# Late stages of a gated hybrid layer: three sets of places for split weights, split two units ahead

## The chip, the cores and the metric

One core of one Trainium2 chip runs the kernel. The metric is the device time in microseconds of one execution. Five engines work side by side, each through its own instructions in order: TensorE (PE, matmuls and its weight loads), VectorE (DVE), ScalarE (ACT), GpSimd (POOL) and SyncE (SP, which here only issues transfers). Matmuls write PSUM, which has eight banks of 128 x 512 floats; everything else stands in SBUF.

## What is computed

One decoder layer on 512 positions of width 2048, in float32. Three token mixers share one input projection; each result is multiplied by SiLU of its gate path, projected back, weighted by a sigmoid gate and summed:

```python
hn = rms_norm(x, norm_gain)
proj = hn @ w_in            # queries, keys, values, z gates, and 3 x 2048 gate_logits
ua = (ya * silu(za)) @ w_branch_a
ub = (yb * silu(zb)) @ w_branch_b
uc = (yc * silu(zc)) @ w_branch_c
g = sigmoid(gate_logits.reshape(b, s, 3, 2048))
y = g[:, :, 0] * ua + g[:, :, 1] * ub + g[:, :, 2] * uc
return x + y @ w_out
```

## The kernel before

**Precision.** Every float32 operand is split into a high piece (ACT's cast to the fast float32 format, "hi") and a low piece (DVE's subtraction of hi from the original, "lo"). A product is three matmuls into one PSUM bank: x-high by w-high, x-low by w-high, x-high by w-low.

**The late stages**, from 714 us on, are a list of units, `late.units`, run one after another by `Late.run`:
- Gates: six blocks (three gates, two halves of 1024 columns). A block is a 2 x 2 block product done with seven products in place of eight. Eight units "FIRST" (F0 to F7 below: products P1, P5, P6, P4, 24 matmuls each), then eight units "SECOND" (S0 to S7: P2, P7, P3, 18 matmuls). Each product has two PSUM banks (two halves t), filled over eight units. In the eighth, each finished product is taken over ("evacuated") by DVE additions into R (`first_1`, `second_2`), P1 by ACT. `tags` rotates the four pairs of banks: in the next block P5 takes the banks of P2, P6 those of P7, and P4 those of P3.
- Branches: four column groups, each branch B (3 units), A (3), C (2), 24 matmuls a unit. In a branch's last unit DVE multiplies by the gate values g, which come back from memory. Four PSUM banks are used in turn with four.
- Output: left block (SECOND, then FIRST), right block (FIRST, then SECOND).

**A unit's weights.** `load` fetches them into a raw tile (three in all); `sums` makes block sums in place on DVE (three subtractions for FIRST, one for SECOND); `early` has ACT cast the first half (P1 and P5, or P2 and P7), hi0; `split` has DVE make lo0 and ACT cast the second half, hi1; lo1 follows on DVE. In before there are two sets of places for each half: hi0 and lo0 in tags a and c, hi1 and lo1 in b and wd.

**The order is written by hand.** `mm` counts matmuls; each third one is a tick, half a slot. `later(dt, f)` puts f's instructions into the engines' queues dt slots on. So an instruction's place in the queue of DVE or ACT is fixed by its slot, and it waits there in order, together with all behind it. SP's order is made by the compiler. Before, in unit i: load of i+3 and split of i+1 at its start, sums of i+2 half a slot in, early of i+2 two slots in.

**Other steps.** `gates.finish` has ACT do a sigmoid on R and store it to memory (four in each block). `plan_x` starts the late units from the stage before. `Branch.split` also fetched, for a branch's first unit, the gate tiles g into four places of a ring that R uses too (`r_tile`).

Of the kernel before, what the change touches and what calls it, by code (L numbers as in the profile page):

```python
# [13 lines left out]
F32R = mybir.dt.float32r  # L14
# [5 lines left out]
P = 128  # L20
# [23 lines left out]
def tile_hybrid_block(ctx, tc, xT, x, memT, mem, ng, mng, w_in, b_forget, gqa, gka, sinks, gqb, gkb, gqc, gkc,  # L44
                      w_mem, w_a, w_b, w_c, w_out, relm, out):
    nc = tc.nc
    ve, ac, po, pe, sy = nc.vector, nc.scalar, nc.gpsimd, nc.tensor, nc.sync
# [7 lines left out]
    def f32(ap):  # L55
        return ap.bitcast(F32)
# [9 lines left out]
    def place(n, name, dtype=F32):  # L66

        return yp.tile([P, 2, S], dtype, tag=f"ys{n}", name=name)
# [43 lines left out]
    gdr = [nc.dram_tensor(f"gates_{i}", (S, D), F32, kind="Internal").ap() for i in range(3)]  # L112
# [9 lines left out]
    def at_slot(t, f):  # L122

        heapq.heappush(agenda, (t, next(seq), f))

    def later(dt, f):
        at_slot(clock[0] + dt, f)
# [42 lines left out]
    def w_tile(which, dtype=F32R):  # L170

        return wp.tile([P, 2, 512], dtype, tag=f"w{which}", name=f"w{which}{cnt[0]}")
# [33 lines left out]
    def bank(i, name):  # L206
        return ps.tile([P, 512], F32, tag=TAGS[i], name=name)
# [92 lines left out]
    early = tc.tile_pool(name="early", bufs=1)  # L300
# [247 lines left out]
    def split(dst_hi, dst_lo, src):  # L548
        ac.copy(dst_hi, src)
        def low():  # L550
            ve.tensor_tensor(dst_lo, src, f32(dst_hi), op=ALU.subtract)
            release("T")
        later(0.5, low)
# [411 lines left out]
    gp = []  # L965
# [6 lines left out]
    def tiles_of(t):  # L972

        return slice(t * P, (t + 1) * P), slice(2 * P + t * P, 2 * P + (t + 1) * P)
# [3 lines left out]
    def r_tile(name):  # L978
        ring["R"] += 1
        return place((0, 1, 2, 6)[ring["R"] % 4], f"{name}_{ring['R']}")  # L980
# [9 lines left out]
    def parts(hi, lo, src, dt=0.5):  # L990
        ac.copy(hi, src)
        later(dt, lambda: ve.tensor_tensor(lo, src, f32(hi), op=ALU.subtract))

    def x_tiles(u, name):
        ax[u] = tuple(cp.tile([P, 4, 256], F32R, tag=f"a{p}{u}", name=f"x{p}{name}{u}") for p in "hl")
        return ax[u]

    def y_tiles(u, name):
        ay[u] = tuple(gp[0].tile([P, 3, 256], F32R, tag=f"b{p}{u}", name=f"y{p}{name}{u}") for p in "hl")
        return ay[u]  # L1000
# [34 lines left out]
    class Late:  # L1035
# [11 lines left out]

        def run(self, lo, hi):
            for i in range(lo, hi):
                self.step("load", i + 3)  # L1050
                self.step("split", i + 1)
                later(0.5, lambda: self.step("sums", i + 2))
                later(2, lambda: self.step("early", i + 2))
                self.units[i].run()

    late = Late()
    wcnt = [0]

    def raw_tile():
        wcnt[0] += 1  # L1060
        return gp[0].tile([P, 4, 512], F32, tag="raw", bufs=3, name=f"rawl{wcnt[0]}")

    def halves():

        n = wcnt[0]
        return ((w_tile("a"), w_tile("c")), (w_tile("b"), gp[0].tile([P, 2, 512], F32R, tag="wd", bufs=2, name=f"wd{n}")))

    def mm(count, *args, **kw):
        pe.matmul(*args, **kw)  # L1069
        count[0] += 1  # L1070
        if count[0] % 3 == 0:
            tick()

    class Product:
# [27 lines left out]

        def half(self, n):

            hi, lo = halves()[n]
            some = sorted(wa for m, xa, wa in (SECOND if self.second else FIRST)[2 * n:2 * n + 2])
            k = len(some)
            src = self.raw[:, some[0]:some[-1] + 1:max(some[-1] - some[0], 1), :]
            ac.copy(hi[:, :k, :], src)  # L1109
            for i, wa in enumerate(some):  # L1110
                self.w[wa] = (hi[:, i, :], lo[:, i, :])
            return lambda: ve.tensor_tensor(lo[:, :k, :], src, f32(hi[:, :k, :]), op=ALU.subtract)  # L1112
# [3 lines left out]

        def split(self):
            self.low()
            later(1.5, self.half(1))

        def run(self):
            u = self.u
# [101 lines left out]
    def plan_x(left):  # L1224


        def alpha(u):
            xs = place(2 + u % 2, f"xa{u}").rearrange("p k (t n) -> p (k t) n", t=2)
            sy.dma_start(out=xs, in_=xad[u * P:(u + 1) * P, :].rearrange("p (k n) -> p k n", n=256))
            later(5, lambda: parts(*x_tiles(u, "x"), xs, 1))  # L1230

        def beta(u):
            if u % 2 == 0:
                beta.t = raw_tile()
            xs = beta.t[:, 2 * (u % 2):2 * (u % 2) + 2, :].rearrange("p k (t n) -> p (k t) n", t=2)[:, 0:3, :]
            sy.dma_start(out=xs, in_=xbd[u * P:(u + 1) * P, :].rearrange("p (k n) -> p k n", n=256))
            later(5, lambda: parts(*y_tiles(u, "x"), xs, 1))
        t0 = left - 32
        for u in range(NP):
            later(max(0, t0 - 16 + 2.5 * u), lambda u=u: beta(u))  # L1240
            later(t0 - 0.5 + 4 * u, lambda u=u: alpha(u))
        for dt, what, i in ((11, "load", 0), (15, "load", 1), (19, "load", 2), (21, "sums", 0), (23, "sums", 1), (25, "sums", 2),
                            (28, "early", 0)):
            later(t0 + dt, lambda what=what, i=i: late.step(what, i))
        later(left - 2.5, lambda: late.step("split", 0))
        later(left - 0.5, lambda: late.step("early", 1))

    def gates(gi, cpair):
        c = cpair * 1024

        def finish(h, t, r):
            def fin():
                ac.activation(r, r, AF.Sigmoid)
                ac.dma_start(out=gdr[gi][tiles_of(t)[h], c:c + 1024].rearrange("p (a n) -> p a n", a=2), in_=r)
            later(4, fin)
        turn = 3 * (len(late.units) // (2 * NP))
        tags = [(turn + n) % 4 for n in range(4)]
        b = Blocks(w_in, GATE + gi * D + c, (tags, tags), finish)
        b.plan(0, b.first_1)
        b.plan(1, b.second_2)  # L1260
# [7 lines left out]
    BR = (("B", w_b, 3, 1, 0), ("A", w_a, 3, 0, 3), ("C", w_c, 2, 2, 6))  # L1268
# [21 lines left out]
    class Branch:  # L1290
# [15 lines left out]

        def split(self):
            br, w, npair, gi, base = BR[self.bi]
            self.hi, self.lo = halves()[(self.cg * 8 + base + self.p) % 2]
            parts(self.hi, self.lo, self.raw[:, 0:2, :], 1)  # L1310
            if self.p == 0:
                for i in range(2):
                    t = r_tile(f"g{br}")
                    sy.dma_start(out=t, in_=gdr[gi][i * 2 * P:(i + 1) * 2 * P, self.cg * 512:(self.cg + 1) * 512]
                                 .rearrange("(b p) n -> p b n", p=P))
                    self.g[2 * i], self.g[2 * i + 1] = t[:, 0, :], t[:, 1, :]

        def run(self):
            br, w, npair, gi, base = BR[self.bi]
            xh, xl = y_split[base + self.p]  # L1320
            first, last = self.p == 0, self.p == npair - 1
            if first:
                self.banks["tags"] = tags = ((2, 3), (0, 1))[ucnt[0] % 2]
                for b in range(4):
                    self.banks[b] = bank(tags[b // 2], f"u{br}{self.cg}_{b}")
                ucnt[0] += 1
            count = [0]
            for b in range(4):
                c = slice(b * P, (b + 1) * P)
                for k in range(2):  # L1330
                    for i, (x, wt) in enumerate(((xh, self.hi), (xl, self.hi), (xh, self.lo))):
                        mm(count, self.banks[b], x[:, k, c], wt[:, k, :], start=(first and k == 0 and i == 0),
                           stop=(last and k == 1 and i == 2))
                if last:
                    self.evac(b)
            if self.cg == 3 and last and self.bi == 0:
                plan_y()
# [18 lines left out]
    def plan_y():  # L1356

        def one(u):
            xs = blocks(place(3 + u % 2, f"ya{u}"))
            sy.dma_start(out=xs, in_=yad[u * P:(u + 1) * P, :].rearrange("p (k n) -> p k n", n=256))  # L1360
            later(5, lambda: parts(*x_tiles(u, "y"), xs, 1))
        for u in range(6):
            later((1, 3, 8, 10, 15, 17)[u], lambda u=u: one(u))
# [34 lines left out]
    for cg in range(4):  # L1398
        for bi, (br, w, npair, gi, base) in enumerate(BR):
            banks, g = {}, {}  # L1400
# [5 lines left out]
    def outputs(cpair, tags):  # L1406
        c = cpair * 1024
        cols = slice(c, c + 1024)

        def finish(h, t, r):  # L1410
            (ac if h else sy).dma_start(out=out[tiles_of(t)[h], cols].rearrange("p (a n) -> p a n", a=2), in_=r)
        return Blocks(w_out, c, tags, finish, resid=x)

    left = outputs(0, ((1, 2, 3, 0), (2, 3, 0)))
# [101 lines left out]
```

## Time and profile before

| | us |
|---|---|
| median of 3 runs | 1533.58 (1532.06 to 1534.87) |
| the profiled execution | 1534.17 |
| its span, first to last instruction | 1532.4 |
| PE busy in the span | 1492.3 |
| DVE busy | 1083.6 |
| ACT busy | 721.6 |

A matmul's end is modelled, so successive rows overlap; the pace is read from the starts. "Idle before" is the time an engine stood before a row, with what ended the wait.

### The profile page before, as it was taken

The page shows a single profiled execution, that of the slowest core. Times are in us where ns is not written, and L with a number is a line of the kernel's source. Part 1 is how long each engine was busy: PE and PEld are TensorE (multiplying, and loading weights), DVE is VectorE, ACT ScalarE, POOL GpSimd, SP SyncE. Part 2 cuts the span into 40 slices and gives each one's busy share as a digit, 9 for nine tenths or more (in the row PEclk, how much of TensorE's full clock was granted, in tenths as well). Part 3 has the DMA queues.
Part 4 walks back from the last instruction along what each step waited for, and adds up shares of the span by engine and source line. Part 5 has one row for each costly group of instructions (what it writes and reads, how often), then busy time and mean ns, then how long its engine had stood idle before and what let it go on. Part 6 is the DMA issues. An engine that isn't in the chain of part 4 may idle for free.

```text
span 1532.4 us, 20507 instructions
## 1 busy us (share of the span) xinstructions
PE 1492.3 (97%) x7233; PEld 1273.4 (83%) x7233; DVE 1083.6 (71%) x1818; ACT 721.6 (47%) x1198; POOL 272.0 (18%) x295
## 2 busy tenths in 40 slices
PE   8999999999999999999999999999999999999998
PEld 7999999998877888888887878787878788887876
DVE  7576765663577764568878877777777556589987
ACT  5434654663566654454444444435355322245432
POOL 3323760662225431200000000000000101110000
PEclk9999999999999999999999999999999999999999
DMA  6656433223244322476666676767676756567583
GB/s 198 172 187 207 122 109 111 84 76 93 83 146 158 99 72 78 162 235 210 210 202 221 206 230 197 243 192 246 193 228 208 278 194 198 173 229 259 191 294 140
DMA packets 125264, 273.23 MB, mean 178 GB/s; under 512 B 13916, under 2 KB 52956, under 8 KB 125160
## 3 DMA queue, kind: packets, MB, share of 16 engines
q1 hardware_dynamic: 120984, 257.22, 52.6%
q10 hardware_dynamic: 4176, 14.69, 3.0%
q8 instruction: 57, 0.93, 0.2%
q14 instruction: 47, 0.39, 0.1%
HBM read 240.39 MB, written 31.48 MB: 177 GB/s over the span
## 4 chain that ended last, share of the span: by engine, by line
PE 73%; DVE 11%; ACT 6%; DMA 5%; issue 3%; POOL 1%; ACTq 1%; SPq 0%; DVEq 0%; POOLq 0%
PE P L1069 27%; PE z L284 11%; PE uA L1069 4%; PE qA L284 4%; PE kB L284 3%; PE qB L284 3%; PE uB L1069 3%; PE kvA L284 3%; PE uC L1069 3%; DMA rawl<-in_w_in_dram 3%; PE qC L284 3%; PE vB L284 2%; DVE R L1003 2%; DVE rawl L1006 2%; DVE wd L1112 2%
## 5 line engine op out<-in xcount | busy, mean ns | idle before, releaser
L1109 ACT CAST wa<-rawl 128x1024 fp32r<-128x1024 f32 x128 | 134.7, 1052 | 256.2 <-PE P L1069 140.1
L198 DVE TENSOR_TENSOR wc<-wa,wb 128x512 fp32r<-128x512 f32 (+2 forms) x254 | 162.0, 664 | 109.3 <-ACT wb L195 108.7
L195 ACT CAST wb<-wa 128x512 fp32r<-128x512 f32 (+2 forms) x254 | 131.3, 565 | 143.8 <-PE z L284 48.3
L1006 DVE TENSOR_TENSOR rawl<-rawl 128x512 f32<-128x512 f32 x256 | 176.6, 690 | 26.6 <-DMA rawl<-in_w_in_dram 16.5
L1112 DVE TENSOR_TENSOR wc<-rawl,wa 128x1024 fp32r<-128x1024 f32 x128 | 156.3, 1221 | 50.8 <-ACT wa L1109 50.7
L1350 POOL TENSOR_TENSOR y<-y,gA 128x512 f32<-128x512 f32 x16 | 24.8, 1559 | 701.0 <-DVE gA L1348 700.4
L1109 ACT CAST wb<-rawl 128x512 fp32r<-128x512 f32 (+1 forms) x128 | 107.1, 837 | 74.7 <-PE P L1069 51.7
L1112 DVE TENSOR_TENSOR wd<-rawl,wb 128x512 fp32r<-128x512 f32 (+1 forms) x128 | 121.8, 952 | 12.9 <-ACT wb L1109 12.7
L284 PE MATMUL z<-ah,wb 128*128 128x512 f32 x256 | 102.2, 399 | 0.0
L284 PE MATMUL z<-ah,wc 128*128 128x512 f32 x256 | 100.0, 391 | 0.0
L284 PE MATMUL z<-al,wb 128*128 128x512 f32 x256 | 99.8, 390 | 0.0
L1069 PE MATMUL P<-wd,xhx 128*128 128x512 f32 x192 | 76.5, 398 | 4.0 <-DVE wd L1112 3.6
L1069 PE MATMUL P<-wb,xhx 128*128 128x512 f32 x192 | 75.9, 395 | 1.8 <-ACT wb L1109 1.0
L1069 PE MATMUL P<-wb,xlx 128*128 128x512 f32 x192 | 74.9, 390 | 0.0
L1069 PE MATMUL P<-wa,xlx 128*128 128x512 f32 x192 | 74.7, 389 | 0.0
L1069 PE MATMUL P<-wa,xhx 128*128 128x512 f32 x192 | 74.7, 389 | 0.0
L1069 PE MATMUL P<-wa,yhx 128*128 128x512 f32 x192 | 74.7, 389 | 0.0
L1069 PE MATMUL P<-wa,ylx 128*128 128x512 f32 x192 | 74.7, 389 | 0.0
L1069 PE MATMUL P<-wc,yhx 128*128 128x512 f32 x192 | 74.7, 389 | 0.0
L1069 PE MATMUL P<-wc,xhx 128*128 128x512 f32 x192 | 74.7, 389 | 0.0
L1003 DVE TENSOR_TENSOR R<-P,R 128x512 f32<-128x512 f32 x88 | 56.1, 684 | 20.6 <-PE P L1069 20.2
L574 POOL TENSOR_SCALAR pB<-pB,denB 128x128 f32<-128x128 f32 (+3 forms) x48 | 56.1, 1169 | 49.1 <-DVE denB L573 34.5
(384 smaller groups left out, 4022.1 us busy)
## 6 DMA issues: line engine op xcount, KB each, us to landing
rawl<-in_w_in_dram SPq DMA_DIRECT2D x144, 512.0 KB, 4.4
rawl<-in_w_out_dram SPq DMA_DIRECT2D x48, 512.0 KB, 4.7
wa<-in_w_in_dram SPq DMA_DIRECT2D x63, 384.0 KB, 3.3
wa<-in_w_in_dram SPq DMA_DIRECT2D x64, 256.0 KB, 3.1
rawl<-in_w_in_dram SPq DMA_DIRECT2D x48, 256.0 KB, 4.2
gates<-R ACTq DMA_DIRECT2D x24, 512.0 KB, 7.9
wa<-in_w_in_dram SPq DMA_DIRECT2D x16, 512.0 KB, 3.7
wa<-in_w_mem_dram SPq DMA_DIRECT2D x16, 512.0 KB, 3.4
```

Of the source, the lines that this page charges most:

```text
L195: ac.copy(hi[:, :n], raw[:, i, :n])
L198: ve.tensor_sub(lo[:, :n], raw[:, i, :n], f32(hi[:, :n]))
L284: pe.matmul(pb, a, m, start=b in fresh, stop=last and not todo[b])
L574: po.tensor_scalar(p, p, den[:, 4 + i:5 + i], None, op0=ALU.mult)
L1003: ve.tensor_tensor(out, a, b, op=ALU.add)
L1006: ve.tensor_tensor(out, a, b, op=ALU.subtract)
L1069: pe.matmul(*args, **kw)
L1109: ac.copy(hi[:, :k, :], src)
L1112: return lambda: ve.tensor_tensor(lo[:, :k, :], src, f32(hi[:, :k, :]), op=ALU.subtract)
L1350: po.tensor_tensor(y, y, g, op=ALU.add)
```

## The change

Three sets of places for each half: the first half takes tags a and c for two units of three and both tiles of b for the third; the second half takes new tags wd and we with three tiles each. Per unit i, load is put in for i+4, early for i+2 at the start, split of i+2 one slot in, sums of i+3 two and a half slots in. Branch gate values are fetched by a step of their own, one slot into a branch's last unit but one. A gate block's sigmoids come 3 slots after the evacuation in place of 4. The first units' steps in `plan_x` are moved to suit.

```diff
             for i in range(lo, hi):
-                self.step("load", i + 3)
-                self.step("split", i + 1)
-                later(0.5, lambda: self.step("sums", i + 2))
-                later(2, lambda: self.step("early", i + 2))
+                self.step("load", i + 4)
+                self.step("early", i + 2)
+                later(1, lambda i=i: self.step("split", i + 2))
+                later(2.5, lambda i=i: self.step("sums", i + 3))
                 self.units[i].run()
...
-    def halves():
-
-        n = wcnt[0]
-        return ((w_tile("a"), w_tile("c")), (w_tile("b"), gp[0].tile([P, 2, 512], F32R, tag="wd", bufs=2, name=f"wd{n}")))
+    hcnt = [0, 0]
+
+    def half_tiles(n):
+
+        hcnt[n] += 1
+        if n == 1:
+            return tuple(gp[0].tile([P, 2, 512], F32R, tag=f"w{i}", bufs=3, name=f"w{i}{hcnt[1]}") for i in "de")
+        return (w_tile("b"), w_tile("b")) if hcnt[0] % 3 == 0 else (w_tile("a"), w_tile("c"))
...
-            hi, lo = halves()[n]
+            hi, lo = half_tiles(n)
...
             self.low()
-            later(1.5, self.half(1))
+            later(1, self.half(1))
...
         for dt, what, i in ((11, "load", 0), (15, "load", 1), (19, "load", 2), (21, "sums", 0), (23, "sums", 1), (25, "sums", 2),
-                            (28, "early", 0)):
+                            (27.5, "early", 0), (28.5, "split", 0), (30, "early", 1), (31.5, "load", 3), (32.5, "split", 1)):
             later(t0 + dt, lambda what=what, i=i: late.step(what, i))
-        later(left - 2.5, lambda: late.step("split", 0))
-        later(left - 0.5, lambda: late.step("early", 1))
...
-            later(4, fin)
+            later(3, fin)
...
-            self.hi, self.lo = halves()[(self.cg * 8 + base + self.p) % 2]
+            self.hi, self.lo = half_tiles((self.cg * 8 + base + self.p) % 2)
             parts(self.hi, self.lo, self.raw[:, 0:2, :], 1)
-            if self.p == 0:
-                for i in range(2):
...
+        def fetch_g(self):
+            br, w, npair, gi, base = BR[self.bi]
+            for i in range(2):
+                t = r_tile(f"g{br}")
...
+            if self.p == npair - 2:
+                later(1, self.fetch_g)
```

## Rows read from the trace of the kernel before

**Rows 1.** The page, busy time of the engines, share of the span, instructions.

```profile
PE 1492.3 (97%) x7233; PEld 1273.4 (83%) x7233; DVE 1083.6 (71%) x1818; ACT 721.6 (47%) x1198; POOL 272.0 (18%) x295
```

**Rows 2.** Timeline of PE: start, duration, engine, line, what; in brackets idle time and releaser.

```profile
786.31 0.39 PE L1069 MATMUL P<-wa,yhx 128*128 128x512 f32 x1
786.54 0.39 PE L1069 MATMUL P<-wa,ylx 128*128 128x512 f32 x1
...
794.11 0.50 PE L1069 MATMUL P<-wb,xhx 128*128 128x512 f32 x1 [0.16 <-DVE R L1003]
794.45 0.40 PE L1069 MATMUL P<-wb,xlx 128*128 128x512 f32 x1
```

**Rows 3.** PE's waits from 714 us on: sum, times, longest.

```profile
PE P L1069 <- DVE wd L1112: 7.2, 10, 1.7
PE uA L1069 <- DVE wc L992: 2.4, 1, 2.4
PE P L1069 <- ACT wb L1109: 1.0, 5, 0.2
PE P L1069 <- DVE R L1003: 0.8, 5, 0.2
```

**Rows 4.** Stretches: length, PE's busy time (matmul records), granted clock, DMA share, GB/s.

```profile
714.30:790.30 76.00, 76.00 (x337) 1.00 0.67 215
793.00:820.00 27.00, 26.02 (x110) 1.00 0.75 242
...
950.30:977.30 27.00, 25.30 (x107) 1.00 0.72 236
```

**Rows 5.** Timeline of PE, last gate block, branches and output.

```profile
1180.26 0.39 PE L1069 MATMUL P<-wa,yhx 128*128 128x512 f32 x1
...
1209.12 0.50 PE L1069 MATMUL uA<-wc,ysh 128*128 128x512 f32 x1 [2.41 <-DVE wc L992]
...
1406.52 0.50 PE L1069 MATMUL P<-wd,xhy 128*128 128x512 f32 x1 [1.71 <-DVE wd L1112]
...
1467.37 0.50 PE L1069 MATMUL P<-wd,xhy 128*128 128x512 f32 x1 [0.71 <-DVE wd L1112]
...
1479.67 0.50 PE L1069 MATMUL P<-wd,xhy 128*128 128x512 f32 x1 [1.13 <-DVE wd L1112]
```

**Rows 6.** Timeline of DVE, the same stretches.

```profile
1181.14 0.69 DVE L1003 TENSOR_TENSOR R<-P,R 128x512 f32<-128x512 f32 x1 [3.39 <-PE P L1069]
...
1204.32 2.48 DVE L1345 TENSOR_TENSOR y<-uB,gB 128x512 f32<-128x512 f32 x4 [7.90 <-DMA gB<-gates]
...
1402.61 0.69 DVE L1006 TENSOR_TENSOR rawl<-rawl 128x512 f32<-128x512 f32 x1 [1.86 <-DMA rawl<-in_w_out_dram]
1403.91 1.42 DVE L1006 TENSOR_TENSOR rawl<-rawl 128x512 f32<-128x512 f32 x2 [0.61 <-DMA rawl<-in_w_out_dram]
```

**Rows 7.** Timeline of DVE at the start of the second gate block.

```profile
789.25 1.28 DVE L1003 TENSOR_TENSOR R<-P,R 128x512 f32<-128x512 f32 x2
790.45 1.22 DVE L1112 TENSOR_TENSOR wd<-rawl,wb 128x1024 fp32r<-128x1024 f32 x1
791.58 3.67 DVE L1003 TENSOR_TENSOR R<-P,R 128x512 f32<-128x512 f32 x6
...
796.30 2.14 DVE L1006 TENSOR_TENSOR rawl<-rawl 128x512 f32<-128x512 f32 x3
798.36 1.22 DVE L1112 TENSOR_TENSOR wd<-rawl,wb 128x1024 fp32r<-128x1024 f32 x1
```

**Rows 8.** Timeline of ACT in the same stretch.

```profile
789.05 1.05 ACT L1109 CAST wa<-rawl 128x1024 fp32r<-128x1024 f32 x1 [1.66 <-PE P L1069]
...
797.15 1.05 ACT L1109 CAST wa<-rawl 128x1024 fp32r<-128x1024 f32 x1 [5.69 <-DVE rawl L1006]
798.11 1.06 ACT L1253 ACTIVATE R<-R 128x1024 f32<-128x1024 f32 x1
...
804.01 1.05 ACT L1109 CAST wb<-rawl 128x1024 fp32r<-128x1024 f32 x1 [0.45 <-ACT R L1253]
```

**Rows 9.** DMA issues from 714 us on: count, KB each, median us to landing.

```profile
gC<-gates SPq DMA_DIRECT2D x8, 512.0 KB, 5.7
```

More of the change, by code (lines that the diff above doesn't have):

```diff
@@ L1308, in split @@
             br, w, npair, gi, base = BR[self.bi]
-            self.hi, self.lo = halves()[(self.cg * 8 + base + self.p) % 2]
+            self.hi, self.lo = half_tiles((self.cg * 8 + base + self.p) % 2)
             parts(self.hi, self.lo, self.raw[:, 0:2, :], 1)
-            if self.p == 0:
-                for i in range(2):
[L1313 to L1316, printed above, removed]
+        def fetch_g(self):
+            br, w, npair, gi, base = BR[self.bi]
+            for i in range(2):
+                t = r_tile(f"g{br}")
+                sy.dma_start(out=t, in_=gdr[gi][i * 2 * P:(i + 1) * 2 * P, self.cg * 512:(self.cg + 1) * 512]
+                             .rearrange("(b p) n -> p b n", p=P))
+                self.g[2 * i], self.g[2 * i + 1] = t[:, 0, :], t[:, 1, :]
         def run(self):
```

## The prediction

> **What bounds the kernel now.** Read the page's engine line first [rows 1]: TensorE (PE) is busy 97% of 1532.4 us. Then ask at which pace it runs. Back to back, the matmuls of the late stages start 0.227 us apart [rows 2], though each row is drawn 0.39 long, so three of them (a tick, half a slot of the hand-written order) take 0.68 us, a slot 1.36, a FIRST unit of 24 matmuls 5.44 and a SECOND unit of 18 matmuls 4.08. The change can't touch that pace; all it can win is time in which PE stands. From 714 us on PE waits for four things only, nearly all of it VectorE (DVE) work [rows 3]. A stall costs its idle time plus 0.27: the late matmul's drawn 0.39 would have overlapped its successor by 0.16, and the step after it is 0.34 instead of 0.227, 0.11 more [rows 2].
>
> Where they are: the table by stretches [rows 4] shows 76 us of block 1 with no idle time and 337 matmul records. At each of the five later starts of a gate block, a window of 27 us holds 110 records (107 in the third), where the same pace would give 121: 2.5 us are missing (3.2 in the third), to one record. The steps between the starts, added up beyond 0.227, give 2.3, 2.4, 3.05, 2.35 and 2.5: **12.6 us in the gates**. One stall in the branch stage costs 2.41 + 0.27 = **2.7**, three in the output stage 1.71 + 0.71 + 1.13 + 3 x 0.27 = **4.4** [rows 5]. Some 0.9 more is in steps too short to carry a wait. In all 20.6 us are to be had, 1.3%.
>
> Why PE waits at a block's start: from S7 (last SECOND unit, start 786.31) DVE has to take in eight results in 0.60 us steps and to make the low pieces for the next block as well [rows 7]; on its rows it has no idle time there. F0 starts at 790.39, and its second half's low piece (790.45) stands behind two evacuations, F1's (798.36) behind F2's sums. Then ScalarE (ACT) does four sigmoids and four stores in a row, and the next high piece, F2's second, is cast only from 804.01 to 805.06 [rows 8], with PE already waiting for it. So lo1 arrives late for F1, F2 and F4. It is lead that is missing, not DVE time: a FIRST unit needs 2.05 (sums) + 1.13 + 1.13 (two low pieces) = 4.3 of 5.44 us.
>
> **The change part by part.**
>
> *Three sets, split two units ahead.* No instruction is added or dropped in the block units; the order on DVE and ACT changes. hi0(j) now comes at the start of unit j-2 (was 2 slots later), lo0(j) and hi1(j) one slot into it (was the start of j-1), lo1(j) two slots into it (was 1.5 slots into j-1), sums(j) 2.5 slots into j-3 (was 0.5 into j-2). With two sets a high piece waits for unit j-2 to leave its set: ACT's cast at 789.05 starts 2.74 us into S7, released by PE [rows 8]. With three, the unit before that has to leave it, so the same release comes a whole unit earlier. In steady state that puts lo0(j) at 5.0 us into j-2 and lo1(j) at 2.3 into j-1, against needs at 10.9+0.45 and 8.2: about 6 us of reserve, where before lo1 had 2 to 3.
>
> *What takes its place: the evacuations.* In S7 the DVE queue now holds, in this order: P2's first half, lo0(F1), P2's second, P7's first (two adds), lo1(F1), P7's second (two), sums(F2), P3's first, P3's second. Before, only lo1(F0) stood between P2 and P3 [rows 7]. Banks decide: all eight PSUM banks are in use, and the next block's P4 takes P3's. Times from S7's start: sums(F1) end at 0.3 (hi1(F0) is cast in 1.05 us from S6's start, when its set comes free; lo1(F0) is made 1.1 to 2.3 us into S6, sums(F1) 2.05 later), so DVE is free when P2's first half arrives at 0.88, as in the undisturbed S7 of the last block, start 1180.26, where DVE starts at 1181.14, released by PE [rows 5, 6]. Then 0.88 + 0.60 + 1.13 + 0.60 + 1.20 + 1.13 + 1.20 + 2.05 = 8.79, and P3's first evacuation ends 0.69 later at 9.48. PE wants that bank 3 slots into F0, at 4.08 + 4.08 = 8.16. It waits 1.32 + 0.05 and pays 0.11 after it: **1.5 us per start**, 5 x 1.5 = 7.4. P6's second half wants P7's bank at 7.48, DVE is done at 6.82: no stall. Behind it nothing is late: lo0(F2) is ready at 11.2, needed at 16.9; after the sigmoids (5.9 us with their stores [rows 8], from 9.7, where F2's two casts end) hi0(F3) is done at 16.8, lo0(F3) at 18, needed at 22.4. From FIRST to SECOND: P6's first half is there 2.72 + 0.88 into F7 and taken over in two additions by 4.9, S0's P7 wants the bank at 6.8, no stall, as before. Gates: 12.6 to 7.4, **5.2 won**.
>
> *Transfers four ahead.* There are still three raw tiles, so a load starts when lo1(j-3) has been made, whatever its place in the program. That happens over a unit earlier, so loads start earlier by one unit less what DVE lags. Sums waited for transfers in the output stage (1.86 and 0.61 us at 1402.61, with lo1(F0) queued behind them) [rows 6]. Now lo1(F0) stands ahead of sums(F1), and the transfer has 4 to 5 us more. The three stalls go: **4.4 won**. SyncE's (SP) queue issues the same transfers; what is queued behind a load is the next load, four units from its use.
>
> *Left output block to right: a new stall.* Both are FIRST there, and F7 of the left has evacuations. From F7's start DVE does P1 (0.88), lo0, P1, lo1, sums, then P6: 0.88 + 0.60 + 1.13 + 0.60 + 1.13 + 2.05 = 6.39, end 7.08, and 0.72 + 0.61 later the second, end 8.41. The right block's P5 wants these banks at 6.80, and 0.79 after that start: 0.33 + 0.54 + 2 x 0.11 = **1.1 lost** where before there was none.
>
> *Gate values on their own.* Eight 512 KB fetches per branch kind stay; they move from a unit before the branch to its last unit but one, plus a slot, four slots (5.4 us) ahead of use. SP reaches them earlier, because it waits for nothing of PE's. For the very first branch both tiles still wait for gate stores: before, gB landed at 1204.2, and DVE stood 7.9 us in front of it with lo(A1), the second unit's of branch A, queued behind [rows 6]. It will still land near 1202 to 1204, but lo(A1) is then behind one product only (done by about 1206, PE needs it at 1209) and loads queued behind it on SP have three units of slack. **2.7 won**; if SP's cover were gone, it would be 2.7 again and no more. Later ones: the slowest kind lands a median 5.7 us after its issue [rows 9]; DVE idles where they are late, with 6 us of reserve. Cost 0, bounds 0 to 2.7. Sigmoids a slot earlier in ACT's order: behind hi1(F2) either way, 0.
>
> *Start of the late stage.* Splits 0 and 1 and early 1 move by a slot or so beside x's splits; PE has no idle time in block 1 [rows 4] and lo0(1) has 4.5 us of reserve. Nothing, up to 1 lost.
>
> **Sum.** 5.2 + 4.4 + 2.7 - 1.1 = 11.2 off the profiled execution's 1534.17 (span 1532.4), which lies 0.6 above the median 1533.58: **1522.4 us** by the median.
>
> **Rivals.**
> (a) *All late-stage bubbles go*: evacuations don't cost what I say, because DVE runs ahead of the order I read or banks are freed sooner. Then 12.6 + 4.4 + 2.7 = 19.7 go: 1514. For it: each bubble is a wait for a split; against it: 0.16 us for "DVE R" at 794.11 [rows 2] is such a bank wait already, with less in the queue ahead of it. The Trainium skill (Perfetto Trace Analysis, Optimization Strategy) says that consistent bubbles, the same gap coming back on the engine that should be full, can mean too little SBUF or PSUM for the next tile. By that rule the added SBUF places would end them all; the trace agrees that they come back alike, every 78.7 us, but shows that PSUM is as full.
> (b) *Transfers stay the bound*: three raw tiles, and SP held by stores. The output stalls at 1406 and 1480 and the one at 1209 stay: 2.0 + 1.4 + 2.7 lost again, 1528.6; half of it, 1525.5.
> (c) *No difference*: each us by which DVE is late beyond 0.58 at S7's start adds one at each of five block starts; at 2.8 late the whole gain is gone, 1533.
> (d) *Slower*: DVE's chain closes on itself. In the new order lo0(j) follows sums(j) directly on DVE, with hi0(j) on ACT between them. If hi0 had to wait for all three sums, a FIRST unit would take 2.1 + 0.1 + 1.05 + 1.13 + 1.13 = 5.5 us, more than PE's 5.44, and DVE could never catch up: sums(F1) end 1.4 into S7, the wait for P3's bank is 2.5, and S0's P7 waits 1.9 for P6's. 5 x 2.5 + 6 x 1.9 = 23.9 against 12.6, 11.3 lost, with the rest won 6.0: 1539. It decides where DVE idles over 0.9 us before each lo0 of a FIRST stage. Against it: the first half needs only the first sum, and the ACT cast at 797.15 did start 0.16 after the first of three (796.30 + 0.69), while the other two ran [rows 7, 8].
> That the change doesn't do what it says, the third set never being reached because something else holds the splits back, leaves the gates at 12.6 and gives much the same time as (c); its chance is in (c)'s.
>
> **How the numbers follow.** Forecast 0.52, (a) 0.12, (b) 0.15, (c) 0.11, (d) 0.10. A measurement here tells about 0.2% (3 us) from no change. Faster: forecast, (a), (b) = 0.79; same 0.11; slower 0.10. The range leaves (d) and the end of (a) out and stops at the middle between (b) and (c): 1515 to 1530. The forecast's own range, 1 us of stall per start either way: 1518 to 1527.
>
> **What would show it.** PE's waits for "wd" in the gates gone, and one wait of 1.4 us for "DVE R" 3 slots into each block's first unit instead, five alike; DVE idle before R rather than before wd; no idle at uA's second unit nor at the left block's F1; two short waits for R at the start of the right block. Wrong if PE waits for R more than 2.5 us per start, if DVE has idle gaps before each "wa"-type low piece, or if SP's loads start no earlier.

## The result and the profile after

The changed kernel takes 1524.3 us (median of 5 runs, 1522.29 to 1524.78) where the kernel before took 1533.58 (median of 5 by then). The ratio is 0.9943, with an interval of 0.9928 to 0.9958: 6.4 to 11.0 us less. The forecast was 1522.4, the range 1515 to 1530. The profiled execution took 1524.78, its span 1522.9.

The stages, from the first matmul of one to the first of the next in PE's timeline (us; the output stage ends with the start of the last matmul, and the tail from there is 7.02 in both):

| kernel | late stage starts | gates | branches | output |
|---|---|---|---|---|
| before | 714.23 | 470.1 | 182.3 | 158.75 |
| after | 715.06 | 464.5 | 179.5 | 156.8 |
| won | | 5.6 | 2.75 | 1.95 |

The stages win 10.3 us. The part ahead of them came out 0.8 longer in this execution; its end lay between 711.9 and 716.0 in the profiles of this study, so that is no effect of the change that could be told. The stages themselves repeat well: two kernels below with the same order in the gates gave 464.6 both.

The engine line of the page answers [rows 1]; PE runs the same number of matmuls, in a shorter span:

```profile
PE 1489.1 (98%) x7233; PEld 1279.5 (84%) x7233; DVE 1084.4 (71%) x1818; ACT 717.8 (47%) x1198; POOL 274.5 (18%) x295
```

PE's waits from 700 us on (what it waited for, sum, times, longest) answer [rows 3]. Of four kinds one is left, the one that was smallest before (0.8 us in 5 waits): no low piece is late any more, and what PE waits for is R, the taking over of a PSUM bank.

```profile
PE P L1073 <- DVE R L1003: 7.8, 9, 1.2
```

The three stages as windows, columns as in [rows 4]:

```profile
715.10:1179.60 464.50, 458.41 (x2018) 1.00 0.67 217
1179.60:1359.10 179.50, 179.50 (x818) 1.00 0.66 223
1359.10:1515.90 156.80, 155.11 (x689) 1.00 0.63 211
```

The missing 6.1 us of busy PE in the first line are five idle times of 1.22, and the branch stage has none. The timeline of DVE at the start of the second gate block, after (S7 starts at 787.14, F0 at 791.22; compare [rows 7]), and below it PE's wait at that start:

```profile
784.16 1.23 DVE L1116 TENSOR_TENSOR we<-rawl,wd 128x1024 fp32r<-128x1024 f32 x1
785.30 2.14 DVE L1006 TENSOR_TENSOR rawl<-rawl 128x512 f32<-128x512 f32 x3
788.02 0.69 DVE L1003 TENSOR_TENSOR R<-P,R 128x512 f32<-128x512 f32 x1 [0.57 <-PE P L1073]
788.62 1.22 DVE L1116 TENSOR_TENSOR wb<-rawl,wb 128x1024 fp32r<-128x1024 f32 x1
789.76 1.88 DVE L1003 TENSOR_TENSOR R<-P,R 128x512 f32<-128x512 f32 x3
791.56 1.22 DVE L1116 TENSOR_TENSOR we<-rawl,wd 128x1024 fp32r<-128x1024 f32 x1
792.69 1.28 DVE L1003 TENSOR_TENSOR R<-P,R 128x512 f32<-128x512 f32 x2
793.89 2.13 DVE L1006 TENSOR_TENSOR rawl<-rawl 128x512 f32<-128x512 f32 x3
795.94 0.68 DVE L1003 TENSOR_TENSOR R<-P,R 128x512 f32<-128x512 f32 x1
```

```profile
796.68 0.50 PE L1073 MATMUL P<-wd,xhx 128*128 128x512 f32 x1 [1.22 <-DVE R L1003]
```

Read DVE's lines from the third on: P2's first half, lo0(F1), P2's second with P7's first two additions, lo1(F1), P7's second two, the three sums of F2, and only then P3's first half, done at 796.62. PE starts P4 in that bank 0.06 later. The low pieces stand well ahead: the first line is lo1(F0), done 5.8 us before F0 starts.

### The profile page after: what moved, and what is told of

The parts are those of the page before. It is cut to its first block, busy times and chain, and to the rows that moved or that the text cites. A ratio compares the mean times of both kernels' runs of the same rounds, so it can differ in the third digit from the quotient of the medians.

```text
span 1522.9 us, 20452 instructions
## 1 busy us (share of the span) xinstructions
PE 1489.1 (98%) x7233; PEld 1279.5 (84%) x7233; DVE 1084.4 (71%) x1818; ACT 717.8 (47%) x1198; POOL 274.5 (18%) x295
## 4 chain that ended last, share of the span: by engine, by line
PE 85%; DVE 8%; ACT 3%; issue 2%; DMA 1%; SPq 1%; POOL 1%; DVEq 0%; ACTq 0%; POOLq 0%
PE P L1073 37%; PE z L284 11%; PE uB L1073 4%; PE uA L1073 4%; PE qA L284 4%; PE kB L284 4%; PE vB L284 3%; PE kvA L284 3%; PE uC L1073 3%; PE qC L284 3%; PE qB L284 2%; DVE R L1003 2%; PE mem L284 2%; DVE wc L198 1%; DVE rawl L1006 1%
## 5 line engine op out<-in xcount | busy, mean ns | idle before, releaser
L1116 DVE TENSOR_TENSOR wc<-rawl,wa 128x1024 fp32r<-128x1024 f32 x85 | 104.9, 1234 | 46.1 <-ACT wa L1113 45.9
L1116 DVE TENSOR_TENSOR we<-rawl,wd 128x512 fp32r<-128x512 f32 (+1 forms) x128 | 122.1, 954 | 12.3 <-ACT wd L1113 8.9
L1113 ACT CAST wd<-rawl 128x512 fp32r<-128x512 f32 (+1 forms) x128 | 106.8, 835 | 30.8 <-DVE rawl L1006 17.6
L1073 PE MATMUL P<-we,xhx 128*128 128x512 f32 x192 | 74.7, 389 | 0.0
L1073 PE MATMUL P<-wd,xlx 128*128 128x512 f32 x192 | 74.7, 389 | 0.0
L1116 DVE TENSOR_TENSOR wb<-rawl,wb 128x1024 fp32r<-128x1024 f32 x43 | 52.5, 1222 | 26.4 <-ACT wb L1113 26.2
L574 POOL TENSOR_SCALAR pA<-pA,denA 128x256 f32<-128x256 f32 (+1 forms) x48 | 47.9, 1014 | 88.0 <-DVE denA L573 88.0
L284 PEld LDWEIGHTS z<-ah,wc 128*128 128x128 f32 x256 | 48.1, 188 | 10.3
L284 PEld LDWEIGHTS z<-al,wb 128*128 128x128 f32 x256 | 48.2, 188 | 8.8
L284 PEld LDWEIGHTS z<-ah,wb 128*128 128x128 f32 x256 | 48.2, 188 | 8.8
```

The costliest lines, as they stand in the source:

```text
L284: pe.matmul(pb, a, m, start=b in fresh, stop=last and not todo[b])
L574: po.tensor_scalar(p, p, den[:, 4 + i:5 + i], None, op0=ALU.mult)
```

## The experiments

The main theory: the third set gives the splits their lead; the two-units-ahead order then puts sums(F2) in front of P3's evacuation, and that is the 1.22 us at each start. Rivals: the earlier transfers or the earlier gate fetch bring the gain; or the wait at the bank has another cause. The stages above are compared, in one profiled execution of each; the medians and ratios are of all its runs, against the kernel before.

**One part taken back: transfers three ahead** (from after).

```
-                self.step("load", i + 4)
+                self.step("load", i + 3)
```

> The changed kernel with loads put in three units ahead in the program, as before, all else as changed. Theory (three raw tiles decide, so a load starts when the low piece of the unit three back is made, whatever its place): the loads start within 0.5 us of the same time, 1524 us, within 1.5. Rival (the four in the program is what took VectorE's waits for transfers away): those waits, 26 us in all before, come back and with them 2 to 4 us of the output stage's stalls, 1526 to 1528.

1524.08, ratio 0.9942 [0.9927, 0.9957], gates 464.6, branches 179.6, output 156.9: no difference. The sums' idle time (DVE's groups by line from 715 us on: busy, mean ns, idle before and releasers) is alike in both: 4.6 us in after, of which 0.4 for transfers, and 4.7 and 0.5 here. In the kernel before the same group stood idle 26.4 us, 22.3 of it for transfers. Below are after and the kernel with the third set alone, which follows further down:

```profile
L1006 DVE TENSOR_TENSOR rawl<-rawl 128x512 f32<-128x512 f32 x247 | 170.5, 690 | 4.6 <-DMA rawl<-in_w_out_dram 0.4
```

```profile
L1006 DVE TENSOR_TENSOR rawl<-rawl 128x512 f32<-128x512 f32 x247 | 170.8, 691 | 24.8 <-DMA rawl<-in_w_in_dram 15.1 <-DMA rawl<-in_w_out_dram 5.7
```

So transfers did become earlier, and neither the place of the load in the program nor the third set does it. The new order does: with it and two sets, below, it is 4.2 us and none for transfers. The reading is that low pieces made earlier release the raw tiles earlier.

**One part taken back: gate values fetched with the split again** (from after).

```
+            if self.p == 0:
+                self.fetch_g()
...
-            if self.p == npair - 2:
-                later(1, self.fetch_g)
```

> The changed kernel with the gate values fetched again where a branch's first unit is split, so now two units ahead of the branch. Theory (their tiles come free only when the last gate block's R has been stored, and SyncE's queue waits in order): the weight loads of branch A stand behind the first fetch until about 1190 us and TensorE waits there for 2 to 6 us, 1526 to 1531. Rival (the queue's order lets the loads pass, and the fetch needs no place of its own): 1524, within 1.

1524.48, ratio 0.9939 [0.9924, 0.9954], gates 464.6, branches 179.8, output 157.3. Nothing is lost, as the rival said. SP's timeline of this kernel shows why: the fetch of gB is issued between the same two loads as in after, where it stands at 1185.04 between loads at 1181.14 and 1185.52.

```profile
1180.43 0.37 SPq L1299 DMA_DIRECT2D rawl<-in_w_a_dram  x1
1184.36 0.37 SPq L1319 DMA_DIRECT2D gB<-gates  x1
1184.83 0.50 SPq L1299 DMA_DIRECT2D rawl<-in_w_a_dram  x1
```

**The fetch's move alone** (from before: the fetch becomes fetch_g, called in the last unit but one).

```
-            if self.p == 0:
-                for i in range(2):
...
+            if self.p == npair - 2:
+                later(1, self.fetch_g)
```

> The kernel before with only the gate values fetched on their own, one slot into a branch's last unit but one. Theory (the stall at branch A's second unit came from lo(A1) queued behind products that wait for gB, and gB waits for the last gate store wherever its fetch stands): unchanged, 1533.5 within 1.5, with the wait of 2 to 2.7 us at uA still there. Rival (the fetch is what held up the weights): that wait goes, 1531 or less.

1532.74, ratio 1.0001 [0.9991, 1.001]: no effect. The stall of the second unit of branch A stays, 1.89 us against 2.41 in [rows 5]:

```profile
1210.12 0.54 PE L1069 MATMUL uA<-wc,ysh 128*128 128x512 f32 x1 [1.89 <-DVE wc L992]
```

**The third set alone** (from before: half_tiles as in after; loads, splits, sums and early as before).

```
...
-        return ((w_tile("a"), w_tile("c")), (w_tile("b"), gp[0].tile([P, 2, 512], F32R, tag="wd", bufs=2, name=f"wd{n}")))
...
+        hcnt[n] += 1
+        if n == 1:
+            return tuple(gp[0].tile([P, 2, 512], F32R, tag=f"w{i}", bufs=3, name=f"w{i}{hcnt[1]}") for i in "de")
+        return (w_tile("b"), w_tile("b")) if hcnt[0] % 3 == 0 else (w_tile("a"), w_tile("c"))
...
```

> The kernel before with one thing of the change: three sets of places for each half; queue order, loads and gate fetches as before. Theory (slots fix only the order, and engines run ahead as far as places allow): before P2's evacuation VectorE is done with lo0(F0) and sums(F1) a few us earlier, so it meets S7 without lag; P3's evacuation has only lo1(F0) ahead of it and lo1(F1) comes about 11 us after S7's start against a need at 12.7. Nearly all 12.6 us of the gates go, uA's 2.7 stay (lo(A1) still stands behind the branch's products): 1519 to 1523. Rival (the place in the queue decides, and the third set alone lets nothing start earlier): 1532 to 1534.

1522.93 (1517.7 to 1526.3), ratio 0.9939 [0.9922, 0.9956]; by the medians no different from after. The stages differ, though they are read from the fastest of its six executions (1517.72), and the last experiment bears them out: gates 458.8 (after 464.5), branches 181.4 (179.5), output 156.8. The places alone win 11.3 us in the gates, twice what the whole change wins there; in the branches they are 1.9 behind after, because uA's stall stays. In DVE's timeline (S7 starts at 783.94) sums(F1) are done before S7, DVE idles 1.84 us ahead of P2, and then takes P2, lo1(F0) and the six additions of P7 and P3 with no sums between them:

```profile
780.85 2.13 DVE L1006 TENSOR_TENSOR rawl<-rawl 128x512 f32<-128x512 f32 x3
784.82 1.37 DVE L1003 TENSOR_TENSOR R<-P,R 128x512 f32<-128x512 f32 x2 [1.84 <-PE P L1073]
786.11 1.22 DVE L1116 TENSOR_TENSOR we<-rawl,wd 128x1024 fp32r<-128x1024 f32 x1
787.24 3.67 DVE L1003 TENSOR_TENSOR R<-P,R 128x512 f32<-128x512 f32 x6
```

PE's waits in it, with the bank waits gone:

```profile
PE P L1073 <- DVE we L1116: 1.9, 4, 0.8
PE uA L1073 <- DVE wb L992: 1.5, 1, 1.5
```

**The new order with two sets** (from after).

```
-            return tuple(gp[0].tile([P, 2, 512], F32R, tag=f"w{i}", bufs=3, name=f"w{i}{hcnt[1]}") for i in "de")
-        return (w_tile("b"), w_tile("b")) if hcnt[0] % 3 == 0 else (w_tile("a"), w_tile("c"))
+            return tuple(gp[0].tile([P, 2, 512], F32R, tag=f"w{i}", bufs=2, name=f"w{i}{hcnt[1]}") for i in "de")
+        return w_tile("a"), w_tile("c")
```

> The changed kernel's order with only two sets of places for each half of the split weights. Theory (the order needs the third set): the low pieces stand in VectorE's queue two units ahead but must wait until the unit two back has left its set, with S7's evacuations behind them: lo0(F1) only 3.8 us into S7, P7's second half done at 9.2 against a need at 7.5, P3's at 11.8; some 3.9 us a start in place of 1.5, 1534 to 1540, no faster than before. Rival (the order alone, low pieces ahead of the next sums, took the stalls away): 1524 to 1526.

1582.86, ratio 1.0314 [1.0292, 1.0335]. The direction is as expected, the size is not: 49 us slower than before. The first start shows four waits for R (0.49, 0.31, 1.31, 1.69), 4.9 us with 0.27 for each. Two more costs were not in the expectation: waits of 0.34, 1.20 and 0.36 at the passage from FIRST to SECOND, 2.7 us, and a lower clock. PE around that start, then three windows (length; busy time with records of PE, PEld, DVE, ACT and POOL; granted clock; DMA share; GB/s):

```profile
803.15 0.79 PE L1073 MATMUL P<-wd,xhx 128*128 128x512 f32 x1 [1.69 <-DVE R L1003]
803.74 0.63 PE L1073 MATMUL P<-wd,xlx 128*128 128x512 f32 x1
804.17 0.63 PE L1073 MATMUL P<-we,xhx 128*128 128x512 f32 x1
```

```profile
795.00:803.00 8.00, 4.36 (x16) 2.35 (x14) 7.93 (x12) 1.85 (x2) 0.00 (x0) 0.97 0.57 202
803.70:809.50 5.80, 5.80 (x15) 4.48 (x14) 3.75 (x5) 3.06 (x3) 0.00 (x0) 0.51 0.18 55
809.60:815.00 5.40, 5.40 (x25) 4.48 (x24) 1.83 (x3) 4.12 (x4) 0.00 (x0) 1.00 0.98 289
```

After a stretch in which PE was busy 4.36 of 8 us, the granted clock is 0.51, the 1.2 GHz level, over the next 5.8 us: the matmuls start 0.43 apart instead of 0.227, and 14 such steps cost 2.8 us. The same comes at the other four starts (0.50 there). From the first block start to the next it takes 86.75 us instead of 77.7. This order without its third set is far worse than either kernel.

**Sums behind the evacuations, at the end of every FIRST and SECOND stage** (from after).

```
-                self.step("early", i + 2)
+                later(0.5, lambda i=i: self.step("early", i + 2))
-                later(2.5, lambda i=i: self.step("sums", i + 3))
+                later(self.units[i].sums_at(), lambda i=i: self.step("sums", i + 3))
...
+        def sums_at(self):
+            return 2.5 if self.u < NP - 1 else 3.5 if self.second else 4.5
```

> The changed kernel with one thing moved: in the last unit of a FIRST or SECOND stage the sums of the unit three ahead go into VectorE's queue half a slot after the unit's end, behind its evacuations, not 2.5 slots in (early half a slot into each unit, so that it still follows the sums). Theory (the 1.2 us waits for R at each gate block's start are the 2.05 us of sums ahead of P3's evacuation): all five waits go, P3's first half is done near 7.4 us into S7 against a need at 8.2, and the waits at the start of the right output block go too, 7.4 + 1.7 + 1.1: 1514 to 1516 us. Rival (VectorE is short of time there, wherever the sums stand): the waits come back as waits for low pieces in the next units, 1522 to 1525.

1524.2, ratio 0.994 [0.9927, 0.9952]: no gain, against the theory; the rival's number, but not by its mechanism, since PE still waits for R: 5.6 us in 7 waits for DVE, 1.6 in 3 for ACT. The gates win 1.6 us (462.9), the output loses 1.9 (158.7). DVE's timeline shows why the waits at the gates' starts stay (S7 starts at 786.30): the sums that F7 had put off end 2.18 into S7, so P2's first half starts 1.2 later than in after. The delay at one end was carried into the other.

```profile
786.34 2.14 DVE L1006 TENSOR_TENSOR rawl<-rawl 128x512 f32<-128x512 f32 x3
788.39 0.68 DVE L1003 TENSOR_TENSOR R<-P,R 128x512 f32<-128x512 f32 x1
```

**The same at the end of the gates' SECOND stages alone** (from after; as above, but):

```
+        def sums_at(self):
+            last = self.u == NP - 1
+            return 3.5 if last and self.done.__name__ == "second_2" else 2.5
```

> As sums_behind, but the sums are moved behind the evacuations in the last SECOND unit of each gate block alone; in the last FIRST units they stay 2.5 slots in. sums_behind kept waits for R of 0.4 to 1.2 us because VectorE came 1.9 us later to S7 (sums(F1) ended 2.2 us into it, not 0.3). Theory (that lag came from the sums moved in F7, where the SECOND units' chain sums, cast, low piece can't make it up; the wait at P3 itself is only the sums ahead of it): VectorE is at S7 as in the changed kernel, the five waits go, 7.4 less, 1516 to 1518. Rival (VectorE has no time left at a block's start, so any order gives the wait to another instruction): 1522 to 1525.

1517.96, ratio 0.9905 [0.989, 0.992]. Gates 457.0: all five waits are gone, by moving the three subtractions of the sums behind P3's additions. That shows the cause of the 1.22 us. The output stage took 159.0 instead of 156.8, because the high piece, half a slot later in every unit here, now stands behind the cast of a y piece on ACT, and DVE stands before its low piece; 13 us later PE waits twice for ACT's copies of R, 0.28 and 0.67, which it doesn't in after. ACT, then DVE:

```profile
1371.18 0.84 ACT L991 CAST yhy<-y4s 128x768 fp32r<-128x768 f32 x1 [2.42 <-DVE y4s L1006]
1371.92 1.05 ACT L1117 CAST wa<-rawl 128x1024 fp32r<-128x1024 f32 x1
```

```profile
1373.00 1.22 DVE L1120 TENSOR_TENSOR wc<-rawl,wa 128x1024 fp32r<-128x1024 f32 x1 [1.85 <-ACT wa L1117]
```

**And at the end of the left output block's FIRST stage too** (from after; as the last one, but):

```
+            return 3.5 if last and self.done.__name__ == "second_2" else 4.5 if last and self.done.__name__ == "first_2" else 2.5
```

> As sums_behind_second, and the sums also moved behind the evacuations in the last FIRST unit of the left output block, whose next unit is FIRST too. Theory: the two waits for R at the right block's start, 1.7 us in the changed kernel, go as well, 1.7 less than sums_behind_second. Rival: VectorE's lag comes back as longer waits for R at the right block's own last FIRST unit (1.1 us now): no difference.

1520.32, ratio 0.9921 [0.9907, 0.9934]: 2.4 us worse than the last one by the medians. The two waits at the right block's start are gone, but at its passage to SECOND the waits grow from 1.23 to 2.32 us, and the output is 159.2 (PE's timeline):

```profile
1477.73 0.50 PE L1073 MATMUL P<-wa,yhy 128*128 128x512 f32 x1 [0.63 <-ACT R L1176]
1481.03 0.50 PE L1073 MATMUL P<-wa,yhy 128*128 128x512 f32 x1 [1.33 <-DVE R L1003]
1482.35 0.50 PE L1073 MATMUL P<-wa,yhy 128*128 128x512 f32 x1 [0.36 <-DVE R L1003]
```

uA's stall is back as well (1.34 us; branches 181.2): DVE's first product came 21.8 us after the first branch matmul here, 19.2 in after. The edit isn't the cause, because up to the output stage every engine runs the same instructions in the same order as in the last kernel; gB landed later in this execution. By the stages 1.65 us are lost in the branches and 0.2 in the output, so the edit gains nothing, and that it costs something isn't shown.

**Both lessons: sums behind, high piece first again** (from after). Only behind a gate block's last SECOND unit do the sums wait until 3.5 slots, and only in the unit after it does the high piece go half a slot later, behind them.

```
-                self.step("early", i + 2)
+                later(0.5, lambda i=i: self.step("early", i + 2)) if self.behind else self.step("early", i + 2)
-                later(2.5, lambda i=i: self.step("sums", i + 3))
+                u = self.units[i]
+                self.behind = getattr(u, "u", 0) == NP - 1 and u.done.__name__ == "second_2"
+                later(3.5 if self.behind else 2.5, lambda i=i: self.step("sums", i + 3))
```

> As sums_behind_second, but early stays at each unit's start and moves half a slot only in the one unit after postponed sums. sums_behind_second took 7.5 us off the gates (457.0 from first matmul to the branches) and added 2.2 to the output stage (159.0 against 156.8), where ScalarE's cast of a first half, half a slot later, stood behind the cast of a y piece that waited for a transpose. Theory (that half slot is the cause): gates 457.0, branches 179.5, output 156.8, 1516 to 1517.5 us. Rival (the output stage is longer because the gates end with VectorE or the transfers in another place): output stays at 159, 1518.

1516.1 (1515.51 to 1517.04), ratio 0.9886 [0.9869, 0.9902]: 8 us faster than after, and the fastest kernel of the study. Gates 457.0, branches 179.5, output 156.4, so the half slot was what the output had lost. The window of the gates (columns as in the three windows above) has no idle PE, and in DVE's timeline the sums of F2 follow four additions instead of two:

```profile
713.80:1170.80 457.00, 457.00 (x2017) 378.38 (x2017) 377.27 (x465) 207.57 (x229) 0.00 (x0) 1.00 0.70 221
```

```profile
790.34 1.22 DVE L1119 TENSOR_TENSOR we<-rawl,wd 128x1024 fp32r<-128x1024 f32 x1
791.47 2.48 DVE L1003 TENSOR_TENSOR R<-P,R 128x512 f32<-128x512 f32 x4
793.86 2.14 DVE L1006 TENSOR_TENSOR rawl<-rawl 128x512 f32<-128x512 f32 x3
```

**Third set, old order, and splits two ahead in the branches only** (from the kernel with the third set alone).

```
+                if n_gates - 3 < i < n_branch - 2:
+                    later(1, lambda i=i: self.step("split", i + 2))
```

> As three_sets_old_order (gates 458.8, branches 181.4, output 156.8), with one more thing of the change: branch units split two units ahead, one slot into the unit. Theory (the branch stall is the low piece of branch A's second unit behind the products that wait for gB): that piece then stands behind one product, the wait of 1.5 us goes or shrinks to what gB's landing leaves, branches 179.5 to 180.5, 1 to 2 us less than three_sets_old_order. Rival (the branches' 1.9 us come from the loads or the gate fetch): 181.4 as there.

1518.12 (1517.53 to 1519.78), ratio 0.9898 [0.9884, 0.9913]. Branches 179.5 and no wait at uA: the split two units ahead wins the 1.9 us that the third set alone left there (the fetch of g moves a unit ahead with it, which was worth nothing above). In the three kernels without this split the stall goes with gB: first product 20.0, 19.5 and 19.1 us after the first branch matmul, stall 2.41, 1.89 and 1.54. Gates 459.2, output 156.3, in an execution near the median (1518.59). So with the old order in the gates the kernel is 6 us faster than after by the medians, with intervals that don't meet, and what the third set wins there is confirmed. PE's waits:

```profile
PE P L1075 <- DVE we L1118: 2.8, 4, 1.0
```

## Why the prediction was right, and where it was not

**The gates.** The step held to the hundredth: P3's first evacuation was put 9.48 us after S7's start, and it ended 796.62 - 787.14 = 9.48 after it. PE's start in that bank was put 1.37 late, and it is 1.38 late (796.68 against 787.14 + 8.16), which the profile draws as 1.22 of idle time. With the longer step behind it a start costs 1.49 against 1.5; five of them 7.45 against 7.4. Predicted 5.2 won, measured 5.6; the rest are steps too short to carry a wait. That it is the sums in front of P3 that cost this was shown by moving them behind it: 464.5 to 457.0. ACT's cast in the next unit moved half a slot with them, since it must follow them; it stands in another queue, and no run moved it alone.

What the prediction didn't see is that its two causes have opposite signs. It asked what the new order costs, but never what the third set would give under the old one: 11.3 us, of 12.6 counted as lost, so that the order gives back 5.6 in the gates. Beside rival (a) stood the rule in the Trainium skill (Perfetto Trace Analysis, Optimization Strategy) that a bubble that comes back alike can mean too little SBUF or PSUM. The trace agrees twice: SBUF places alone ended all but one (0.59 us) of the waits for low pieces in the gates, and what the new order put there was a wait for a PSUM bank, alike at each of five starts. The chance of (a) was low for the right reason, though: not places, but the queue in front of a bank, kept this kernel from 1514; with the queue mended it was 1516.1.

**The branches.** 2.7 predicted, 2.75 measured, by the reason in part. lo(A1) behind one product was right, and that comes from the split's order; the fetch of its own, which stood in the same paragraph, is worth nothing in either direction (1524.48 with it taken back, 1.0001 alone). The spare in front of uA was thinner than said, too. DVE waits for gB as before (after, DVE's timeline; compare [rows 6]):

```profile
1198.75 0.69 DVE L1350 TENSOR_TENSOR y<-uB,gB 128x512 f32<-128x512 f32 x1 [8.32 <-DMA gB<-gates]
1199.35 1.22 DVE L992 TENSOR_TENSOR wb<-rawl,wb 128x1024 fp32r<-128x1024 f32 x1
```

The first product comes 19.2 us after the first branch matmul (before 20.0), and lo(A1) is done at 21.0, needed at 22.2: 1.2 us to spare where 3 were expected. A fetch that lands 2.6 later uses that up, as happened in one experiment whose edit doesn't touch the branches. That all 2.7 were won here is luck in part.

**The output.** The 4.4 went as said; no wait for a low piece is left. The stage's gain doesn't hang on the earlier transfers, though: with the third set alone the sums stand idle for the output's transfers nearly as long as before (5.7 us against 5.8), three waits for low pieces stay, 1.34 us in place of 3.55, and the output takes the same 156.8. The new stall at the right block's start was there, in the two places named, but 0.80 + 0.36 + 0.54 = 1.7 instead of 1.1. The mis-sized term is the first addition: it was put 0.88 us into the left block's F7 (start 1431.64) and came at 1.49, because ACT first copies the same result, P1, out of that bank into another quarter of R. PE, ACT and DVE of after:

```profile
1439.40 0.50 PE L1073 MATMUL P<-wb,xhy 128*128 128x512 f32 x1 [0.80 <-DVE R L1003]
1440.72 0.50 PE L1073 MATMUL P<-wb,xhy 128*128 128x512 f32 x1 [0.36 <-DVE R L1003]
...
1484.07 0.50 PE L1073 MATMUL P<-wa,yhy 128*128 128x512 f32 x1 [0.17 <-DVE R L1003]
1485.39 0.50 PE L1073 MATMUL P<-wa,yhy 128*128 128x512 f32 x1 [0.36 <-DVE R L1003]
```

```profile
1432.52 0.59 ACT L1212 COPY R<-P 128x512 f32<-128x512 f32 x1 [1.36 <-PE P L1073]
```

```profile
1433.13 0.69 DVE L1003 TENSOR_TENSOR R<-P,R 128x512 f32<-128x512 f32 x1 [1.75 <-ACT R L1212]
...
1474.64 0.69 DVE L1006 TENSOR_TENSOR rawl<-rawl 128x512 f32<-128x512 f32 x1 [0.38 <-DMA rawl<-in_w_out_dram]
...
1476.58 1.23 DVE L1116 TENSOR_TENSOR wc<-rawl,wa 128x1024 fp32r<-128x1024 f32 x1 [1.25 <-ACT wa L1113]
...
1480.26 1.23 DVE L1116 TENSOR_TENSOR wb<-rawl,wb 128x1024 fp32r<-128x1024 f32 x1 [1.25 <-ACT wb L1113]
```

The last two PE lines, 1.07 us, were not foreseen: the passage from FIRST to SECOND of the right block. The prediction had worked that passage out in the gates alone, and called it free there. The last two DVE lines show what came in front of it: in these units DVE stands 1.25 us before a low piece, for the cast of a high piece that itself waits for the sum. That is the chain of rival (d), which was sought in FIRST units and shows in SECOND units; that it makes DVE late for the two evacuations is read from the order of these lines, and no run took it alone. The first of the two waits has another part: ahead of these units DVE stands 0.38 us for a transfer (1474.64), and over three kernels with this order that idle time and PE's wait rise together (0.38, 0.52, 0.88 and 0.17, 0.34, 0.73); in the fastest kernel, which has no such idle time, only the 0.36 is left. Predicted 4.4 - 1.1 = 3.3, measured 1.95; the two misses are 0.6 and 1.07, and 0.3 are small steps the other way. In all, 11.2 us were forecast and the stages won 10.3; the miss lies in the output.

**The reserves.** The text put lo1(j) 2.3 us into unit j-1 and spoke of 6 us of reserve. The first row of the DVE timeline after puts lo1(F0)'s end at 785.39, 2.3 us into S6, which is unit j-2, and 8.5 us ahead of F0's second half. Behind a block's start DVE lags, and there the text is near: lo1(F3) is done at 806.49, 2.9 us into F2, with 5.7 to spare. So j-1 holds for some units and not for F0; no number of the sum rested on it.

**The rivals.** (b) fell: the group of sums stands idle 4.6 us instead of 26.4, with the same three raw tiles. (c) fell: DVE was free 0.57 us ahead of P2 in S7. (d) has its chain, and with it one of the prediction's signs of being wrong: DVE stands 1.25 us before the first half's low piece in 45 of the 64 SECOND units. In the FIRST units, on which (d) rested, it stands in 5 of 64, behind the sigmoids. In the gates PE waits for none of it; in the output it is part of 1 us.

## What to carry to other kernels

A split that is made earlier is one more job in the queue of the engine that also empties PSUM; write that queue out for the unit in which the banks change hands, and put work that nothing needs yet behind the evacuations. Separate the places from the order: here three sets alone won 11.3 us in the gates, the order that came with them gave 5.6 back, and a few lines that moved three subtractions won 7.5 there. Where two edits come as one, ask of each what it would do without the other, and look for the buffer that releases a transfer before moving its line in the program.

## What the runs showed of the hardware

The clock was the surprise. In the kernel with two sets, four waits one after the other (0.49, 0.31, 1.31 and 1.69, PE busy 4.36 of 8 us) were followed by a stretch of 5.8 us at a granted clock of 0.51, the 1.2 GHz level, with matmuls 0.43 us apart. In after, single waits of 1.22 us left the gates at 1.00. The other finding is the bank that ACT and DVE both read: DVE's addition started only when ACT's copy out of it was done, 0.6 us later than PE's result allowed. Whether the chip asks for that or the program's own waits do, no run here shows.
